# Weight blocks of a two-layer fp32 trunk: six of them split into a rounded part and its remainder by transfers instead of a subtraction on VectorE

## The chip, the cores and the metric

The kernel runs on one core of one Trainium2 chip. The metric is the device time of one execution in microseconds, as a median of several runs: 1206.23 us for the kernel before (three runs, 1202.98 to 1206.3 us). A profile is one further execution, recorded by the hardware profiler; every duration below is from that execution.

## The reference

A trunk of two layers works on x (512 positions by 1024 channels) and on a memory of 256 positions. Each layer has a mixer, an attention over the memory and a squared-ReLU MLP, each behind an RMS norm and added to x:

```python
mem_n = rms_norm(mem, mem_norm_g)
for l in range(2):
    h = rms_norm(x, mix_norm_g[l])
    x = x + (mixer_attn_rglru(h, ...) if l % 2 == 0 else pool_mixer(h, pool_w, scale))
    x = x + memory_xattn(rms_norm(x, xattn_norm_g[l]), mem_n, w_q, w_kv, q_g, k_g, w_o)
    x = x + jnp.square(jax.nn.relu(rms_norm(x, mlp_norm_g[l]) @ w1)) @ w2
```

The part of interest is layer 1. Its pooling mixer forms, in four groups of 256 channels, the mean over the last 2, 4, 8 or 16 positions minus the value itself, after which each group goes through a 256x256 matrix:

```python
window_sum = cs[:, 1:, sl] - cs[:, lo, sl]
diffs.append(window_sum / count - hf[..., sl])
out = jnp.einsum('bsgc,gcd->bsgd', d, pool_w)
```

The memory attention of the same layer needs k and v of the memory, `mem_n @ w_kv` with a weight of 1024 x 2048. This product doesn't depend on x, so it can be computed beside the mixer. All arithmetic is fp32.

## The kernel before

**Three products for one.** TensorE multiplies in a rounded fp32 type (fp32r). To keep fp32 accuracy, each operand is split into a high part (the value rounded to fp32r) and a low part (the value minus its high part), and `mm3` (L361) adds three matmuls: high x high, high x low, low x high. A weight comes from memory in blocks of 128 x 1024 fp32 (512 KB). `conv` (L427) splits a block: `split` (L383) has ScalarE (ACT) write the high part `wh` from the raw block, and then has VectorE (DVE) write the low part `wl` = `raw` - `wh`. An activation or norm operand is split in the same way (`xh`, `xl` and others).

**Buffers.** Raw blocks lie in a ring of 8 buffers that SP's queue fills (L394), each load waiting for the subtraction that frees its buffer. `wh` and `wl` have 5 buffers each; `block()` (L450), which TensorE's code calls for the next block, starts the split of the block that lies four further on. In the MLPs some raw blocks are added to others in memory: a transfer issued by GpSimd (POOL) with `accum_op=add` (L415), 128 of them in the program.

**Order.** The order on every engine is made when the program is built, and it is fixed: each engine takes its instructions one after the other, and each waits for the semaphores of what it reads or overwrites. The order comes from a small planner. Every operation asks for its engine (`yield ("dve", ...)`), and of those whose inputs are due soon, `tick` (L206) takes the one with the earliest due block; the table `DUE` (L20) holds how many blocks ahead of its use each kind of work is due.

**Layer 1 around the change.** `run` (L1490) sets the order of TensorE's blocks. Block numbers count weight blocks in the order in which TensorE takes them, from 0:

- blocks 173 to 176: the first quarter of `w_kv` (k of heads 0 and 1)
- blocks 177 and 178: the pooling matrices (`pool_mix`, L1436), 24 matmuls of 512 columns each
- blocks 179 to 190: the other three quarters of `w_kv` (`kv_group`, L1093), 12 matmuls of 512 columns each
- blocks 191 and on: the query projection, 24 matmuls each, which reads x after the mixer

While TensorE works through blocks 179 to 190, VectorE does what follows the pooling matrices for the eight tiles m = 0 to 7 of x: it scales the product (`z`), forms the window sums (`zs`, for m of 4 and more from a running sum `zc`), the difference `df`, adds it to `x`, and then splits the new x for the query projection: ScalarE writes `xh`, VectorE `xl` (L570). ScalarE and VectorE also square and add x for the next norm (`sq`), and finish k (`ksq`, `xss`, `xvv` and, over GpSimd's power `xrk`, `xkn`, which TensorE transposes into `kTh`, `kTl`) and v (`xvh`, `xvl`).

Of the kernel before, what the change touches and what calls it, by code (L numbers as in the profile page):

```python
# [6 lines left out]
F32 = mybir.dt.float32  # L7
F32R = mybir.dt.float32r
AF = mybir.ActivationFunctionType
ALU = mybir.AluOpType  # L10
# [6 lines left out]
WARM = 12  # L17
MM = 0.2162 / 512

DUE = {'xv': 0.3, 'xg': 2.6, 'xw': 4.9, 'evac_s': 0.6, 'form': 1.6, 'late': 2.5, 'stats_d': 2.31, 'exact': 0.32, 'q2': 8.88, 'conv': 1.47, 'evac': 1.41, 'norm': -1.9, 'sq': 3.08, 'stats': 0.76, 'xc0': 9.87, 'xc1': 1.14, 'gate0': 17.89, 'gate1': 1.73, 'kt': 15.09, 'qt': 13.77, 'dil0': 15.42, 'dil1': 2.26, 'lru': 6.84, 'pool0': 131.7, 'pool1': 1.91, 'soft': 2.17, 'kvt': -0.68, 'mem': 32.21, 'o': 2.22, 'conv_d': 0.31, 'mem_d': 56.21, 'lam_d': 2.23}  # L20
LOOK = 0.33
BACK = 0.46
TABLE = 1.28
# [22 lines left out]
def weight_blocks():  # L46

    out = []

    def cols(name, l, c0, k0=0, nk=4):  # L50
        for j in range(nk):
            out.append((name, l, k0 + 256 * j, c0))

    cols("ev_w_in", 0, 1536)
    cols("ev_w_in", 0, 512)
    cols("ev_w_in", 0, 0)
    out.append(("gates", 0, 0, 0))
    cols("ev_w_in", 0, 1024)
    cols("ev_w_in", 0, 2048)

    def kv(l, g0, g1):
        for g in range(g0, g1):
            cols("xa_w_kv", l, 512 * g)

    def two(name, l):
        cols(name, l, 0)
        cols(name, l, 512)

    def mlp(l):
        for c in range(4):  # L70
            for g in range(2):
                for i, j in S_RAWS:
                    out.append(("s:mlp_w1", l, 512 * j, 1024 * c + 512 * g + 256 * i))
            for g in range(2):
                for i, j in S_RAWS:
                    out.append(("t:mlp_w2", l, 1024 * c + 256 * j, 512 * g + 256 * i))

    kv(0, 0, 4)
    two("ev_w_out", 0)
    two("xa_w_q", 0)  # L80
    two("xa_w_o", 0)
    mlp(0)
    kv(1, 0, 1)
    out.append(("pool", 0, 0, 0))
    out.append(("pool", 0, 1, 0))
    kv(1, 1, 4)
    two("xa_w_q", 1)
    two("xa_w_o", 1)
    mlp(1)
    return out  # L90
# [5 lines left out]
def weight_units():  # L96


    out = []
    b, at = 0, 0.0  # L100
    blocks = weight_blocks()
    while b < NBLK:
        if blocks[b][0][1] == ":":
            for f in FORMS:
                for g in range(2):
                    out.append((b + 4 * g, f, at, 4 / 7))
                    at += 4 / 7
            b += 8
        else:
            out.append((b, None, at, 1))  # L110
            at += 1
            b += 1
    return out


UNITS = weight_units()


def weight_loads():


    out = []
    for b, form, _, _ in UNITS:
        if form in (None, "11"):
            out.append((b, (b, form), None))
        elif form == "a":
            out.append((b + 1, (b, form), b + 2))
        elif form == "c":
            out.append((b + 1, (b, form), b))
        elif form in ("12", "22"):  # L130
            out.append((b + (3 if form == "12" else 2), (b, form), None))
    return out


LOADS = weight_loads()
ACCUM = 7.9


class Trunk:
# [96 lines left out]
    def due_at(self, block):  # L236
        self.cur[1] = block
# [161 lines left out]
    def dma_next(self):  # L399

        if self.n_dma < len(LOADS) and self.n_raw < RAW_BUFS - 1:
# [6 lines left out]
            if more is not None:  # L408
                u = self.unit_at[key]
                self.spawn(self.accum(raw, more, f"F{u}"), UNITS[u][2] - DUE["conv"])  # L410

# [11 lines left out]
    def raw_free(self):  # L423
        self.n_raw -= 1
        self.dma_next()

    def conv(self, u):  # L427

        b, form, _, _ = UNITS[u]
        if form in ("a", "b", "c", "d"):  # L430
            yield f"F{u}"
        src = self.raw[b, {"b": "a", "d": "a"}.get(form, form)]
        hi = self.p_w.tile([128, 1024], F32R, tag="wh", name="wh")
        lo = self.p_w.tile([128, 1024], F32R, tag="wl", name="wl")
        self.w[u] = (hi, lo)
        if isinstance(src, list):
            for k in range(2):
                c = slice(512 * k, 512 * k + 512)
                yield from self.split(hi[:, c], lo[:, c], src[k])
        else:  # L440
            yield from self.split(hi, lo, src)
        self.mark(f"w{u}")
        if form in ("a", "b"):

            self.spawn(self.accum(src, b + (0 if form == "a" else 3), f"F{u + 4}", hi, lo),
                       UNITS[u + 4][2] - DUE["conv"])
        elif not isinstance(src, list):
            self.raw_free()

    def block(self):  # L450

        u = self.unit
        self.unit += 1
        self.blk = UNITS[u][2] + UNITS[u][3]
        if self.n_conv < len(UNITS):
            n = self.n_conv
            self.spawn(self.conv(n), UNITS[n][2] - DUE["conv"], DUE["conv_d"])
            self.n_conv += 1
        self.need(f"w{u}")
        return self.w.pop(u)  # L460


    def gemm_t(self, xs, evac, between=None, groups=2, nkb=4, tail=None):


        for g in range(groups):
            ps = [None] * 4
            for j in range(nkb):
# [5 lines left out]
                for m, k in order[:6] if last else order:  # L474
# [11 lines left out]
                    if kk == 2 * nkb - 1:  # L486
                        self.spawn(evac(4 * g + m, ps[m]), self.blk - DUE["evac"])
                    self.tick()
# [17 lines left out]
    def gemm_s(self, ops, evac, tail=None):  # L506
# [6 lines left out]
        for form in FORMS:  # L513
            for g in range(2):
# [22 lines left out]
                if not last:  # L537
                    self.spawn(evac(g, form, ps, gid), self.blk - DUE["evac_s"])

# [5 lines left out]
    def gemm_n(self, xs, nt, evac, nkb=4):  # L545

        ps = [None] * nt
        for j in range(nkb):
            wh, wl = self.block()
            for t in range(nt):  # L550
                if j == 0:
                    ps[t] = self.acc()
                for k in range(2):
# [6 lines left out]
                    if kk == 2 * nkb - 1:  # L560
                        self.spawn(evac(t, ps[t]), self.blk - DUE["evac"])
                    self.tick()
# [1025 lines left out]
```

## Time and profile before

| what | us |
|---|---|
| median of the runs | 1206.23 |
| the profiled execution, its own time | 1208.11 |
| its span, first to last instruction | 1206.3 |
| TensorE (PE) busy | 1186.3 |
| weight loads into TensorE (PEld) busy | 1093.1 |
| VectorE (DVE) busy | 931.9 |
| ScalarE (ACT) busy | 666.8 |
| GpSimd (POOL) busy | 148.8 |

The profiled execution's own time is 1.8 us above its span. Busy shares are averages over stages; what a stage waits for is read from the rows of that stage. A busy time of TensorE counts matmuls that run at a lower granted clock as busy too.

### The profile page before, as it was taken

How to read it: one execution, taken by the hardware profiler on the slowest of the kernel's cores; microseconds unless marked ns; L12 is line 12 of the kernel's file. 1: busy time of each engine (PE TensorE's matmuls, PEld its weight loads, DVE VectorE, ACT ScalarE, POOL GpSimd, SP SyncE). 2: the span in 40 equal slices, each digit the busy share in tenths (PEclk: the TensorE clock that was granted, in tenths of full speed). 3: DMA queues.
4: the chain of work that ended last, by engine and by line, in shares of the span. 5: the costliest groups of instructions: out<-in, count | busy, mean ns of one | idle time of the engine just before them, and what ended most of it. 6: DMA issues, size and time to landing. Idle time of an engine off the chain costs nothing.

```text
span 1206.3 us, 19988 instructions
## 1 busy us (share of the span) xinstructions
PE 1186.3 (98%) x7984; PEld 1093.1 (91%) x7984; DVE 931.9 (77%) x1419; ACT 666.8 (55%) x965; POOL 148.8 (12%) x172
## 2 busy tenths in 40 slices
PE   9999999999999999999999999999999999999998
PEld 6887888888889999999999977788899999999998
DVE  7959885555569877858958999946599869699697
ACT  6487764444456746436536657444476456465462
POOL 0110010010101111121211010001011211212110
PEclk9999999999999999999999999999999999999999
DMA  9223253322438699799899644433477998998984
GB/s 365 80 93 110 87 179 106 105 87 70 101 92 206 158 265 237 172 259 242 192 249 234 181 156 142 140 88 70 105 172 196 231 239 219 257 242 208 247 210 105
DMA packets 58989, 208.03 MB, mean 172 GB/s; under 512 B 6672, under 2 KB 7184, under 8 KB 58896
## 3 DMA queue, kind: packets, MB, share of 16 engines
q1 hardware_dynamic: 40320, 139.59, 33.2%
q0 software_dynamic: 18432, 67.12, 30.9%
q8 instruction: 62, 1.02, 0.3%
q14 instruction: 31, 0.25, 0.1%
q10 hardware_dynamic: 144, 0.05, 0.0%
HBM read 204.63 MB, written 2.10 MB: 171 GB/s over the span
## 4 chain that ended last, share of the span: by engine, by line
PE 81%; DVE 9%; ACT 4%; DMA 3%; issue 2%; POOL 0%; SPq 0%; DVEq 0%; ACTq 0%; POOLq 0%
PE acc L366 50%; PE misc L366 28%; DMA raw<-wpack 3%; DVE wl L274 3%; PE misc L373 1%; DVE p L274 1%; PE misc L379 1%; ACT wh L264 1%; DVE x L274 1%; DVE fl L274 1%; ACT sq L264 1%; DVE sq L274 1%; ACT xh L264 0%; DVE hs L274 0%; ACT a L264 0%
## 5 line engine op out<-in xcount | busy, mean ns | idle before, releaser
L264 ACT ACTIVATE wh<-raw 128x1024 fp32r<-128x1024 f32 (+1 forms) x321 | 333.4, 1049 | 297.2 <-PE acc L366 120.3
L274 DVE TENSOR_TENSOR wl<-raw,wh 128x1024 fp32r<-128x1024 f32 (+1 forms) x321 | 387.2, 1212 | 140.5 <-ACT wh L264 140.1
L415 POOL DMA_DIRECT2D raw<-wpack x128 | 111.2, 871 | 639.4 <-DVE wl L274 375.0
L366 PE MATMUL acc<-fh,wl 128*128 128x256 f32 x448 | 127.8, 285 | 3.7 <-DVE wl L274 3.7
L366 PE MATMUL acc<-fl,wh 128*128 128x256 f32 x448 | 127.6, 285 | 0.5 <-DVE x L274 0.5
L366 PE MATMUL misc<-fl,wh 128*128 128x256 f32 x448 | 127.1, 284 | 1.0 <-DVE fl L274 1.0
L366 PE MATMUL misc<-fh,wl 128*128 128x256 f32 x448 | 126.9, 283 | 0.8 <-DVE wl L274 0.8
L366 PE MATMUL acc<-fh,wh 128*128 128x256 f32 x448 | 127.5, 285 | 0.0
L366 PE MATMUL misc<-fh,wh 128*128 128x256 f32 x448 | 126.8, 283 | 0.0
L366 PEld LDWEIGHTS acc<-fh,wl 128*128 128x128 f32 x448 | 86.7, 194 | 4.3 <-DVE wl L274 4.3
L366 PEld LDWEIGHTS misc<-fl,wh 128*128 128x128 f32 x448 | 86.0, 192 | 1.6 <-DVE fl L274 1.6
L366 PEld LDWEIGHTS acc<-fl,wh 128*128 128x128 f32 x448 | 86.7, 193 | 0.7 <-DVE x L274 0.7
L366 PEld LDWEIGHTS misc<-fh,wl 128*128 128x128 f32 x448 | 86.0, 192 | 1.0 <-DVE wl L274 1.0
L366 PEld LDWEIGHTS acc<-fh,wh 128*128 128x128 f32 x448 | 86.6, 193 | 0.0
L366 PE MATMUL acc<-xh,wh 128*128 128x512 f32 x208 | 82.8, 398 | 3.4 <-ACT xh L264 2.2
L366 PEld LDWEIGHTS misc<-fh,wh 128*128 128x128 f32 x448 | 86.0, 192 | 0.0
L366 PE MATMUL acc<-xh,wl 128*128 128x512 f32 x208 | 82.1, 395 | 1.4 <-DVE wl L274 1.4
L366 PE MATMUL acc<-xl,wh 128*128 128x512 f32 x208 | 82.5, 397 | 0.8 <-DVE xl L274 0.8
L366 PE MATMUL acc<-oh,wh 128*128 128x512 f32 x160 | 62.7, 392 | 0.7 <-ACT oh L264 0.7
L366 PE MATMUL acc<-oh,wl 128*128 128x512 f32 x160 | 62.8, 392 | 0.0
L366 PE MATMUL acc<-ol,wh 128*128 128x512 f32 x160 | 62.5, 391 | 0.2 <-DVE ol L274 0.2
L366 PE MATMUL acc<-wl,mh 128*128 128x512 f32 x128 | 50.8, 397 | 0.9 <-DVE wl L274 0.9
(288 smaller groups left out, 3212.2 us busy)
## 6 DMA issues: line engine op xcount, KB each, us to landing
raw<-wpack SPq DMA_DIRECT2D x253, 512.0 KB, 4.8
raw<-wpack POOLq DMA_DIRECT2D x128, 512.0 KB, 6.9
x<-xT SPq DMA_DIRECT2D x8, 256.0 KB, 5.6
outT<-x SPq DMA_DIRECT2D x6, 256.0 KB, 2.2
raw<-wpack SPq DMA_DIRECT2D x4, 256.0 KB, 4.9
memr<-memT SPq DMA_DIRECT2D x4, 256.0 KB, 3.8
cst<-cst SPq DMA_DIRECT2D x1, 617.0 KB, 6.8
outT<-x SPq DMA_DIRECT2D x4, 128.0 KB, 2.4
```

The source lines that it names most:

```text
L264: self.nc.scalar.activation(out, in_, func, **kw)
L274: getattr(self.nc.vector, fn)(out, *args, **kw)
L366: self.nc.tensor.matmul(out, a, b, start=start and i == 0, stop=stop and i == 2, skip_group_check=shared)
L373: self.nc.tensor.transpose(out, in_, self.ident)
L379: self.nc.tensor.matmul(ps[:, t:t + 1], sq[:, t * 128:t * 128 + 128], self.one, start=True, stop=True)
L415: self.nc.gpsimd.dma_start(out=raw, in_=self.ins["wpack"][b], accum_op=ALU.add)
```

## The change

Six of the twelve blocks 179 to 190 are split in another way. They are the blocks of `w_kv` in layer 1, from column 512 on, whose rows begin at 256 or 768: blocks 180, 182, 184, 186, 188 and 190, every other one.

For such a block, GpSimd's queue issues a transfer of the block from memory straight into `wh`, which rounds it to fp32r on the way. ScalarE then writes `wl` = -1 x `wh`, and a second transfer on GpSimd's queue adds the block from memory to `wl`, which leaves the block minus its high part. The raw ring, the load on SP's queue and VectorE's subtraction are not used for these blocks. The table DUE gets one more entry, `'direct': 3.0`, the lead in blocks with which the planner counts these splits as due (1.47 for the others).

```diff
+def direct(block):
+
+    name, l, r0, c0 = block
+    return name == "xa_w_kv" and l == 1 and c0 >= 512 and r0 % 512 == 256
+
+
 def weight_loads():
...
+    blocks = weight_blocks()
     for b, form, _, _ in UNITS:
         if form in (None, "11"):
-            out.append((b, (b, form), None))
+            if not direct(blocks[b]):
+                out.append((b, (b, form), None))
...
+    def put(self, out, b, ins, key=None, **kw):
+
+        yield ("pool", ins)
+        self.nc.gpsimd.dma_start(out=out, in_=self.ins["wpack"][b], **kw)
+        t = max([self.free["dma"], self.T] + [self.due[r.tensor.name][0] for r in ins])
+        self.free["dma"] = max(self.free["dma"], self.T) + 524288 / 360e3
+        self.free["pool"] = max(self.free["pool"], self.T) + 0.9
+        self.due[out.tensor.name] = (t + ACCUM, "dma")
+
+    def conv_direct(self, u, b):
+
+        hi = self.p_w.tile([128, 1024], F32R, tag="wh", name="wh")
+        lo = self.p_w.tile([128, 1024], F32R, tag="wl", name="wl")
+        self.w[u] = (hi, lo)
+        yield from self.put(hi, b, [])
+        yield from self.A(lo, hi.bitcast(F32), AF.Copy, scale=-1.0)
+        yield from self.put(lo, b, [lo], accum_op=ALU.add)
+        self.mark(f"w{u}")
+
     def conv(self, u):
 
         b, form, _, _ = UNITS[u]
+        if form is None and direct(weight_blocks()[b]):
+            yield from self.conv_direct(u, b)
+            return
...
-            self.spawn(self.conv(n), UNITS[n][2] - DUE["conv"], DUE["conv_d"])
+            b, form = UNITS[n][:2]
+            lead = DUE["direct"] if form is None and direct(weight_blocks()[b]) else DUE["conv"]
+            self.spawn(self.conv(n), UNITS[n][2] - lead, DUE["conv_d"])
```

The planner puts the instructions around these blocks in another order. On **VectorE**, the piece that ends with the first update of x tile m = 2 (`x1_86<-df_...`; `x0_85` before it is m = 0 and 1). Before, with the subtractions of blocks 185 and 186 (`wl_7504`, `wl_7531`) in it:

```order
L274 TENSOR_REDUCE xss_7543<-ksq_7546 128x2
L274 TENSOR_TENSOR zs_7515<-z_7388 128x511
L274 SCALAR_TENSOR_TENSOR xvv_7544<-xss_7543,m_e_1400 128x2
L274 TENSOR_REDUCE xss_7558<-ksq_7561 128x2
L274 SCALAR_TENSOR_TENSOR xvv_7559<-xss_7558,m_e_1400 128x2
L274 SCALAR_TENSOR_TENSOR xl_7542<-x0_85,vec_83,xh_7541 128x512
L274 TENSOR_TENSOR zs_7556<-zs_7515 128x510
L274 TENSOR_TENSOR zs_7556<-zs_7556,cst_84 128x4
L274 TENSOR_TENSOR wl_7504<-raw_7347,wh_7503 128x1024
L274 SCALAR_TENSOR_TENSOR df_7595<-zs_7556,z_7388 128x512
L274 TENSOR_TENSOR wl_7531<-raw_7403,wh_7530 128x1024
L274 SCALAR_TENSOR_TENSOR x1_86<-df_7595,vec_83,x1_86 128x512
```

Now the same piece, with the subtraction of block 185 (`wl_7520`) and the two reductions of k's squares (`xss`) behind the update:

```order
L282 TENSOR_TENSOR zs_7494<-z_7388 128x511
L282 SCALAR_TENSOR_TENSOR xl_7509<-x0_85,vec_83,xh_7508 128x512
L282 TENSOR_TENSOR zs_7515<-zs_7494 128x510
L282 TENSOR_TENSOR wl_7520<-raw_7261,wh_7519 128x1024
L282 TENSOR_TENSOR zs_7515<-zs_7515,cst_84 128x4
L282 SCALAR_TENSOR_TENSOR df_7545<-zs_7515,z_7388 128x512
L282 SCALAR_TENSOR_TENSOR x1_86<-df_7545,vec_83,x1_86 128x512
L282 TENSOR_TENSOR sq_7501<-sq_7501,sq_7524 128x512
L282 TENSOR_TENSOR zs_7547<-z_7407 128x511
L282 SCALAR_TENSOR_TENSOR xl_7552<-x1_86,vec_83,xh_7551 128x512
L282 TENSOR_REDUCE xss_7562<-ksq_7565 128x2
L282 TENSOR_REDUCE xss_7576<-ksq_7579 128x2
```

Between the subtraction of block 179 and this update of x, both included, VectorE's list had eight subtractions before (blocks 179 to 186) and has four now (179, 181, 183, 185).

On **ScalarE**, the split of block 184: before, its high part (`wh_7479`) came early, ahead of the first new `xh`.

```order
L264 ACTIVATE wh_7459<-raw_7277 128x1024
L264 ACTIVATE wh_7479<-raw_7309 128x1024
L264 ACTIVATE zs_7486<-z_7374 128x1
L264 ACTIVATE wh_7503<-raw_7347 128x1024
L264 ACTIVATE zs_7515<-z_7388 128x1
L264 ACTIVATE xh_7508<-x0_85,vec_83 128x512
```

Now ScalarE's part of block 184 is the negated copy `wl_7484`, and it stands behind the `xh` of x tile m = 2. (`wh_7459` is block 183 and `wl_7411` the copy of block 182.)

```order
L272 ACTIVATE wh_7459<-raw_7239 128x1024
L272 ACTIVATE zs_7469<-z_7374 128x1
L272 ACTIVATE wl_7411<-wh_7410 128x1024
L272 ACTIVATE xh_7487<-x0_85,vec_83 128x512
L272 ACTIVATE zs_7494<-z_7388 128x1
L272 ACTIVATE sq_7501<-x0_85 128x512
L272 ACTIVATE xh_7508<-x0_85,vec_83 128x512
L272 ACTIVATE zs_7515<-zs_7494 128x2
L272 ACTIVATE wh_7519<-raw_7261 128x1024
L272 ACTIVATE sq_7524<-x0_85 128x512
L272 ACTIVATE xh_7551<-x1_86,vec_83 128x512
L272 ACTIVATE wl_7484<-wh_7483 128x1024
```

The last of the six copies, `wl_7689` of block 190, stands in the same way behind the `xh` of tile m = 5 (the second `xh<-x2_87`), and also behind the high part of block 192 (`wh_7753`):

```order
L272 ACTIVATE wh_7727<-raw_7347 128x1024
L272 ACTIVATE xh_7731<-x2_87,vec_83 128x512
L272 ACTIVATE sq_7750<-x2_87 128x512
L272 ACTIVATE wh_7753<-raw_7403 128x1024
L272 ACTIVATE wl_7689<-wh_7688 128x1024
```

Each of these copies is followed by an adding transfer on GpSimd's queue, which TensorE's low matmuls of the block wait for. GpSimd's list had four `xrk` and nothing else in this stretch; now twelve transfers stand among them.

## Rows read from the trace of the kernel before

**Rows 1.** The page: span and busy times; us, share of the span, instructions.
```profile
span 1206.3 us, 19988 instructions
PE 1186.3 (98%) x7984; PEld 1093.1 (91%) x7984; DVE 931.9 (77%) x1419; ACT 666.8 (55%) x965; POOL 148.8 (12%) x172
```
**Rows 2.** Windows: stretch and length, busy us and count of PE, PEld, DVE, ACT, POOL.
```profile
720.00:740.00 20.00, 20.00 (x94) 16.57 (x93) 18.82 (x31) 15.59 (x27) 1.83 (x2) 1.00 0.50 158
740.00:760.00 20.00, 17.68 (x76) 13.62 (x75) 19.89 (x27) 10.86 (x16) 0.00 (x0) 1.00 0.41 132
```
**Rows 3.** Timeline of PE: start, duration, then [idle before it <- releaser].
```profile
742.89 0.39 PE L366 MATMUL acc<-wh,mh 128*128 128x512 f32 x1
743.72 0.50 PE L366 MATMUL acc<-wl,mh 128*128 128x512 f32 x1 [0.44 <-DVE wl L274]
...
747.24 0.50 PE L366 MATMUL acc<-wl,mh 128*128 128x512 f32 x1 [0.51 <-DVE wl L274]
...
754.62 0.50 PE L366 MATMUL acc<-xh,wl 128*128 128x512 f32 x1 [1.38 <-DVE wl L274]
...
773.11 0.50 PE L366 MATMUL acc<-xh,wh 128*128 128x512 f32 x1 [1.63 <-ACT xh L264]
774.16 0.50 PE L366 MATMUL acc<-xl,wh 128*128 128x512 f32 x1 [0.54 <-DVE xl L274]
```
**Rows 4.** Windows, PE alone: stretch, length, busy us (count), granted clock, DMA share, GB/s.
```profile
488.00:491.00 3.00, 1.00 (x9) 1.00 0.00 0
492.00:496.00 4.00, 4.00 (x23) 0.57 0.81 142
678.00:680.00 2.00, 0.33 (x4) 1.00 0.00 0
680.00:684.00 4.00, 4.00 (x34) 1.00 0.67 192
771.00:775.00 4.00, 1.83 (x8) 1.00 0.53 153
775.00:779.00 4.00, 4.00 (x12) 0.57 0.69 238
```
**Rows 5.** Timeline of PE: first matmuls of blocks 179 and 184.
```profile
717.47 0.39 PE L366 MATMUL acc<-wh,mh 128*128 128x512 f32 x1
...
731.07 0.39 PE L366 MATMUL acc<-wh,mh 128*128 128x512 f32 x1
```
**Rows 6.** Timeline of DVE, 715 to 756 us.
```profile
715.62 1.21 DVE L274 TENSOR_TENSOR wl<-raw,wh 128x1024 fp32r<-128x1024 f32 x1
716.75 0.68 DVE L274 TENSOR_TENSOR z<-acc,R 128x512 f32<-128x512 f32 x1
...
727.97 0.69 DVE L274 TENSOR_REDUCE xss<-ksq 128x2 f32<-128x512 f32 x1 [0.74 <-ACT ksq L264]
...
730.04 0.74 DVE L274 SCALAR_TENSOR_TENSOR xl<-x,vec,xh 128x512 fp32r<-128x512 f32 x1
...
734.47 0.74 DVE L274 SCALAR_TENSOR_TENSOR x<-df,vec,x 128x512 f32<-128x512 f32 x1
...
755.20 0.75 DVE L274 SCALAR_TENSOR_TENSOR x<-df,vec,x 128x512 f32<-128x512 f32 x1
```
**Rows 7.** Timeline of ACT.
```profile
717.49 1.06 ACT L264 ACTIVATE wh<-raw 128x1024 fp32r<-128x1024 f32 x1 [3.11 <-PE acc L366]
...
724.21 0.71 ACT L264 ACTIVATE xh<-x,vec 128x512 fp32r<-128x512 f32 x1
```
**Rows 8.** GpSimd's adding transfers, whole span: duration of the issue; time to landing.
```profile
L415 POOL DMA_DIRECT2D raw<-wpack x128: 862/862/1217, 285.6 to 1179.5; - x128
...
DMA to landing us min/median/max: 5.2/6.9/14.5
```
**Rows 9.** The same, the five that are issued from 640 to 700 us.
```profile
DMA to landing us min/median/max: 5.4/5.6/11.1
```
**Rows 10.** SP's raw loads, 680 to 800 us.
```profile
DMA to landing us min/median/max: 3.4/3.9/5.6
```

More of the change, by code (lines that the diff above doesn't have):

```diff
@@ L18 @@
 MM = 0.2162 / 512
-DUE = {'xv': 0.3, 'xg': 2.6, 'xw': 4.9, 'evac_s': 0.6, 'form': 1.6, 'late': 2.5, 'stats_d': 2.31, 'exact': 0.32, 'q2': 8.88, 'conv': 1.47, 'evac': 1.41, 'norm': -1.9, 'sq': 3.08, 'stats': 0.76, 'xc0': 9.87, 'xc1': 1.14, 'gate0': 17.89, 'gate1': 1.73, 'kt': 15.09, 'qt': 13.77, 'dil0': 15.42, 'dil1': 2.26, 'lru': 6.84, 'pool0': 131.7, 'pool1': 1.91, 'soft': 2.17, 'kvt': -0.68, 'mem': 32.21, 'o': 2.22, 'conv_d': 0.31, 'mem_d': 56.21, 'lam_d': 2.23}
+DUE = {'direct': 3.0, 'xv': 0.3, 'xg': 2.6, 'xw': 4.9, 'evac_s': 0.6, 'form': 1.6, 'late': 2.5, 'stats_d': 2.31, 'exact': 0.32, 'q2': 8.88, 'conv': 1.47, 'evac': 1.41, 'norm': -1.9, 'sq': 3.08, 'stats': 0.76, 'xc0': 9.87, 'xc1': 1.14, 'gate0': 17.89, 'gate1': 1.73, 'kt': 15.09, 'qt': 13.77, 'dil0': 15.42, 'dil1': 2.26, 'lru': 6.84, 'pool0': 131.7, 'pool1': 1.91, 'soft': 2.17, 'kvt': -0.68, 'mem': 32.21, 'o': 2.22, 'conv_d': 0.31, 'mem_d': 56.21, 'lam_d': 2.23}
 LOOK = 0.33
```

## The prediction, made before the changed kernel had run

> **What bounds the kernel now.** I read the page first: the span is 1206.3 us and VectorE is busy 77% of it [rows 1]. An average says little about twelve blocks, so next came the windows by stage. From 740 to 760 us VectorE is busy 19.89 of 20 us, while TensorE, which has work all the time, is busy only 17.68 [rows 2]. So in this stage, and in few others, VectorE sets the pace.
>
> The timeline of TensorE shows what that costs. Five matmuls come late: two low matmuls of blocks 188 and 189, one of block 191, and two that wait for the last split of x [rows 3]. Their idle times add to 0.44 + 0.51 + 1.38 + 1.63 + 0.54 = 4.5 us. Each costs a bit more than its idle: the first pair starts 0.83 us apart, where such matmuls stand 13.60 / 60 = 0.227 us apart (blocks 179 to 183, five blocks of 12, fill 717.47 to 731.07 [rows 5]); 0.83 - 0.227 - 0.44 = 0.16 us more. With that for all five the stage loses 5.3 us.
>
> There is a second loss behind it. After TensorE has idled most of 771 to 775 us, the mean granted clock of 775 to 779 is 0.57 of full speed [rows 4], so it ran most of that stretch at 1.2 GHz instead of 2.4: 4 x (1 - 0.57) = 1.7 us are lost. The same happens after an idle of 2.00 us within 488 to 491 us (0.57 in 492 to 496) and doesn't after 1.67 us within 678 to 680 (1.00 in 680 to 684) [rows 4]. I carry 1.7 us for a wait as long as the two that were followed by it. What the stage loses now: 5.3 + 1.7 = 7.0 us. That is all that a change in this stage can win, if nothing takes its place.
>
> **What the change removes.** Six subtractions of VectorE. One occupies it for 716.75 - 715.62 = 1.13 us (its row shows 1.21, so 0.08 overlap the next; a row of 512 elements, 0.68, occupies it for 0.6) [rows 6]. Together 6.8 us, more than the 5.3 us by which it is late. VectorE's lateness at blocks 188, 189 and 191 and at the last x should therefore go: the whole 7.0 us. Six raw loads leave SP's queue, so its ring reaches further ahead; I found no row of ScalarE in this stage that a load releases, and count nothing.
>
> **What it adds without cost.** Six negated copies replace six high parts on ScalarE, both 128 x 1024 (1.06 us [rows 7]): no difference in busy time. Twelve issues of 0.86 us [rows 8] are 10.3 us for GpSimd, which does 1.83 us of work in 720 to 740 [rows 2]; the `xrk` pair that stands behind block 184's adding transfer has inputs that are themselves later now, so it hides. GpSimd's next powers come after the last of the twelve.
>
> **What it adds on the path: the way to `wl`.** Before, a low part needed ScalarE, then VectorE, some 2.3 us after the raw block was there. Now it needs a rounding transfer, the copy, and an adding transfer, one after the other, and all three stand in queues that take their work in order. The price of an adding transfer, from issue to landing: the fastest of 128 took 5.2 us, their median is 6.9 [rows 8], and the five issued last before this stage have 5.6 [rows 9]. I take 5.8, a little over the nearest row, since twelve more transfers join here. No row shows a rounding transfer: a plain load from SP needs 3.4 us at best [rows 10], an adding one 6.9. Both ends give the same, as the copy behind it waits longer for something else, as follows.
>
> *Block 182* tells how near this runs. Its copy stands behind the high part of block 183, which waits for TensorE to finish block 178, at 717.49 [rows 7]. Copy done 717.49 + 1.06 + 1.06 = 719.6; add landed at 725.4. TensorE wants it one matmul into block 182, at 717.47 + 3 x 2.72 + 0.23 = 725.9. It holds, by 0.5 us.
>
> *Block 184* doesn't. Its copy stands on ScalarE behind `xh` of x tile 2, which waits for VectorE to update that tile. This update started at 734.47 [rows 6]. Four of the subtractions ahead of it go (4 x 1.13 = 4.5 us), and the two `xss` with their wait move behind it: from about 727.2 (727.97 less its wait of 0.74) to 730.04, less one `zs` of 0.6 that stays, 2.2 us [rows 6]. So it starts at 734.47 - 6.7 = 727.8 and ends at 728.5. Then `xh` (0.71) and the copy (1.06 [rows 7]): issue at 730.3. The rounding transfer for this block can be issued right after block 182's add at 719.6 and has landed by 727.4 even at 6.9 us, so it is not what ends last. The add lands at 730.3 + 5.8 = 736.1. TensorE, which nothing else delays, wants it at 731.07 + 0.23 = 731.3 [rows 5]. **TensorE waits 4.8 us**, longer than any wait it has now, and by the rows on the clock pays **1.7 us** more.
>
> *Blocks 186 and 188.* After the wait, block 184 has 11 matmuls left (2.5 us), and the transposes of k (0.9: blocks 184 to 187 took 742.89 - 731.07 = 11.8 us [rows 3, 5], of which four times 2.72 are matmuls). So 185 starts at 739.5 and 190 at 739.5 + 5 x 2.72 = 753.1. The copies for 186 and 188 come to ScalarE at about 735 and 741, so their adds land at about 742 and 748, within 0.7 us of TensorE's need on either side; the 1.7 us of slow clock cover that.
>
> *Block 190* is late again. Its copy stands behind `xh` of tile 5, whose x update was at 755.20, 20.7 us after that of tile 2 [rows 6]. Between the two, three subtractions go (-3.4); the `xss` pair and its small followers come in (+1.3) with one `sq` more (+0.6), one `xvl` moves out (-0.7); and VectorE idles some 1.0 us at k's `kTl`: its transposes stand on TensorE behind the wait at block 184, so with a copy by ScalarE its input is there at 738, and VectorE by the same count at 737. So 727.8 + 18.5 + 1.0 = 747.3, ended 748.0; then `xh`, `sq`, block 192's high part and the copy, by [rows 7] 0.71, 0.6, 1.06 and 1.06 less the overlaps, some 3.2: issue at 751.2, landed 757.0. TensorE wants it at 753.1 + 0.23 + 1.7 = 755.0. **Wait 2.0 us**, and just long enough for **1.7 us** of clock again.
>
> **Sum.** Lost now in this stage 4.8 + 1.7 + 2.0 + 1.7 = 10.2 us, before 7.0: 3.2 us slower. Behind it VectorE has slack (its last x is some 6 us earlier while TensorE is later), and TensorE is the bound, so the 3.2 us go through to the end: 1208.1 + 3.2 = 1211.3 on the profiled execution's scale. The median of the runs lies 1.9 us lower, so 1209.4.
>
> A page speaks against the price that I took. The Trainium skill ("DMA: Bandwidth & Descriptors", Anatomy of one DMA — SWDGE (gpsimd) path) gives a transfer issued by GpSimd as about 2.0 us plus its bytes over 436 GB/s, by estimate 3.2 us for 512 KB. No adding transfer of this trace comes near that: the fastest of 128 needed 5.2. By the page block 184 would wait 2.2 us instead of 4.8; the nearest row that would give such a time is the plain load, which is the second rival.
>
> **Rivals.**
> - *The transfers are slower than the nearest row.* Over the whole span the median add takes 6.9 us, and single ones up to 14.5 [rows 8]. From about 6.3 us block 182 begins to wait, and each microsecond more is paid at block 184 and again at 190, as its copy is late by the idle at `kTl` too. At 6.9: 1.1 x 2 = 2.2 us more plus 0.6 at block 182, so 6.0 us slower, 1212.2; at 8 us 4.4 + 1.7 more, 9.3 us slower, 1215.5. For it: six adds also convert to fp32r, which no row shows, and raw loads share the queues. Against: this stage has the lightest transfer load (share 0.41 to 0.50 [rows 2]).
> - *A GpSimd transfer lands like a plain load*, 3.4 us. Then block 184 waits 730.3 + 3.4 - 731.3 = 2.4 us, clock 1.7; block 190 starts 2.4 us sooner (752.6 with the clock), VectorE has no idle at `kTl`, the add lands at 750.2 + 3.4 = 753.6: wait 1.0. Together 5.1 against 7.0: 1204.3. Against it stand 128 adds of 5.2 us or more.
> - *The relief carries (faster).* If VectorE reaches tile 2's update 3 to 5 us before my sum, block 184's copy is bound by its rounding transfer alone: landed about 725.5, copy, add, 732.4: wait 1.1, no drop, and nothing at block 190. That is 6 us faster, 1200.3. For it: VectorE is the named releaser of most waits. Against: the order fixes what stands ahead of the update.
> - *That the change doesn't do what it says*: the built order has the six subtractions gone and the twelve transfers in, so this is left only as a case with no difference.
>
> **How the numbers follow.** The forecast (adds landing in 5.4 to 6.3 us, 1.5 to 5 us slower; 1207.7 to 1211.2) gets 0.55. A change of less than 0.3%, 3.6 us, can't be told from none here; the bound to slower is 1209.85, so the forecast sits just within, and I give 0.33 of it to no difference and 0.22 to slower. Slow transfers 0.20 (slower). Landing like a plain load 0.12 (0.08 same, 0.04 faster, by the spread of the runs, 3.3 us). The relief 0.09 (faster). No effect 0.04 (same). Faster 0.13, same 0.45, slower 0.42. The range leaves out the relief below and the worst of slow transfers above: 1203.2 to 1215.5.
>
> **What would show it.** Right: a PE row `acc<-wl,mh` that idles 4 to 5.5 us before block 184's second matmul, near 736 us, released by a DMA into `wl`; a shorter one near 757; the clock near half for some microseconds after the first; the five waits of [rows 3] gone; adding transfers at 5.4 to 6.3 us. Wrong: a wait below 3 us at block 184, waits still named after VectorE, or PE busy throughout.

## The result, and the profile after

| | before | after |
|---|---|---|
| median of the runs, us | 1206.26 (1202.98 to 1206.73, six) | 1214.49 (1211.49 to 1215.73, six) |
| ratio to before | 1 | 1.007 (95% interval 1.0055 to 1.0086) |
| the profiled execution, us | 1208.11 | 1214.86 |

The change made the kernel slower by 8.2 us, 0.7%. The forecast was 1209.4, 3.2 slower; the time is inside the range, but it belongs to the first rival, which had a chance of 0.20 ("the transfers are slower than the nearest row": 1212.2 at a landing of 6.9 us, 1215.5 at 8).

The page of after, answering to [rows 1]:

```profile
span 1213.1 us, 19992 instructions
PE 1187.8 (98%) x7984; PEld 1093.8 (90%) x7984; DVE 926.5 (76%) x1413; ACT 666.2 (55%) x965; POOL 157.9 (13%) x184
```

VectorE lost its six subtractions (1419 to 1413 instructions, 5.4 us less busy), and the span grew by 6.8. The execution of before came 2.2 us later to the stage in question, so I measure the stage by itself, between two TensorE rows that every version has: the matmuls of `r`, just ahead of the pooling matrices, and the first scores of the attention behind the query projection (columns as in [rows 3]). Before:

```profile
702.41 1.16 PE L677 MATMUL misc<-cst,r 128*128 128x128 f32 x8 [0.66 <-POOL r L296]
794.12 0.28 PE L366 MATMUL misc<-kTh,qh 128*128 128x256 f32 x1
```

After:

```profile
700.19 1.16 PE L709 MATMUL misc<-cst,r 128*128 128x128 f32 x8 [0.66 <-POOL r L304]
800.99 0.28 PE L374 MATMUL misc<-kTh,qh 128*128 128x256 f32 x1
```

The stage took 91.71 us and now takes 100.80: **9.1 us more: the stage holds the whole loss** (from the scores to the end of the span both executions take 412.1 to 412.2 us). The late matmuls of TensorE from block 179 on, which answer to [rows 3], are the second matmuls of blocks 180, 182, 184, 186 and 190:

```profile
718.62 0.50 PE L374 MATMUL acc<-wl,mh 128*128 128x512 f32 x1 [0.22 <-DMA wl<-wpack]
726.53 0.50 PE L374 MATMUL acc<-wl,mh 128*128 128x512 f32 x1 [2.13 <-DMA wl<-wpack]
734.46 0.50 PE L374 MATMUL acc<-wl,mh 128*128 128x512 f32 x1 [0.57 <-DMA wl<-wpack]
744.27 0.52 PE L374 MATMUL acc<-wl,mh 128*128 128x512 f32 x1 [3.17 <-DMA wl<-wpack]
761.26 0.50 PE L374 MATMUL acc<-wl,mh 128*128 128x512 f32 x1 [4.21 <-DMA wl<-wpack]
```

Not one is released by VectorE or ScalarE any more; all five wait for an adding transfer. The granted clock fell behind three of them (windows of TensorE, columns as in [rows 4]):

```profile
727.00:731.00 4.00, 4.00 (x13) 0.57 0.59 190
744.00:748.00 4.00, 3.73 (x9) 0.58 1.03 235
761.00:765.00 4.00, 3.74 (x10) 0.59 0.69 251
```

That gives the sum again: waits of 10.3 us, some 0.8 around them (0.16 each, as in the prediction), and 4 x (0.43 + 0.42 + 0.41) = 5.0 us of clock are 16.1, against 7.0 before: 9.1.

GpSimd's timeline shows the issues (start, duration), of which six rows:

```profile
717.72 0.87 POOL L438 DMA_DIRECT2D wl<-wpack  x1 [5.88 <-DVE wl L282]
718.48 0.67 POOL L438 DMA_DIRECT2D wh<-wpack  x1
...
729.02 0.88 POOL L438 DMA_DIRECT2D wl<-wpack  x1 [3.99 <-ACT wl L272]
732.26 2.66 POOL L304 TENSOR_TENSOR xrk<-xvv,cst 128x2 f32<-128x2 f32 x2 [2.36 <-DVE xvv L282]
...
737.05 0.89 POOL L438 DMA_DIRECT2D wl<-wpack  x1 [1.58 <-ACT wl L272]
...
753.73 0.87 POOL L438 DMA_DIRECT2D wl<-wpack  x1 [11.00 <-ACT wl L272]
```

and the issues of the stage by tile, adding transfers and then rounding ones, the time to landing:

```profile
L438 POOL DMA_DIRECT2D wl<-wpack x6: 867/878/892, 710.9 to 753.7; - x6
DMA to landing us min/median/max: 5.4/7.5/8.8
```
```profile
L438 POOL DMA_DIRECT2D wh<-wpack x6: 548/600/889, 700.1 to 741.8; - x6
DMA to landing us min/median/max: 3.9/5.0/9.1
```

One by one the adds took 7.6, 8.8, 5.4, 7.2, 7.5 and 7.5 us, each issued 0.3 us behind the end of its copy (block 182's too, where the profile names a subtraction of VectorE that ended 0.2 us later than the copy). The longest is block 182's: a rounding transfer was issued right behind it at 718.48, and took 9.1.

### The profile page after: what moved, and what is told of

It reads as the page before. It is cut to its first block, busy times and chain, and to the rows that moved or that the text cites. A ratio compares the mean times of both kernels' runs of the same rounds, so it can differ in the third digit from the quotient of the medians.

```text
span 1213.1 us, 19992 instructions
## 1 busy us (share of the span) xinstructions
PE 1187.8 (98%) x7984; PEld 1093.8 (90%) x7984; DVE 926.5 (76%) x1413; ACT 666.2 (55%) x965; POOL 157.9 (13%) x184
## 4 chain that ended last, share of the span: by engine, by line
PE 82%; DVE 6%; DMA 5%; ACT 4%; issue 2%; POOL 0%; SPq 0%; DVEq 0%; ACTq 0%; POOLq 0%
PE acc L374 52%; PE misc L374 28%; DMA raw<-wpack 3%; DMA wl<-wpack 2%; DVE wl L282 2%; PE misc L381 1%; DVE p L282 1%; PE misc L387 1%; ACT wh L272 1%; DVE fl L282 1%; DVE x L282 1%; DVE hs L282 0%; ACT a L272 0%; PE misc L709 0%; ACT sq L272 0%
## 5 line engine op out<-in xcount | busy, mean ns | idle before, releaser
L282 DVE TENSOR_TENSOR wl<-raw,wh 128x1024 fp32r<-128x1024 f32 (+1 forms) x315 | 380.3, 1213 | 149.5 <-ACT wh L272 149.1
L272 ACT ACTIVATE wh<-raw 128x1024 fp32r<-128x1024 f32 (+1 forms) x315 | 327.2, 1049 | 303.5 <-PE acc L374 126.5
L374 PE MATMUL acc<-wl,mh 128*128 128x512 f32 x128 | 52.7, 412 | 10.3 <-DMA wl<-wpack 10.3
```

The source lines that it names most:

```text
L272: self.nc.scalar.activation(out, in_, func, **kw)
L282: getattr(self.nc.vector, fn)(out, *args, **kw)
L374: self.nc.tensor.matmul(out, a, b, start=start and i == 0, stop=stop and i == 2, skip_group_check=shared)
```

## The experiments

Theories, by the letters that the expectations use. **A**: the way to the low part (rounding, copy, add) is too long, and the adds land last. **B**: the new order of VectorE's and ScalarE's work is what makes TensorE late, whatever the transfers do. **C**: the twelve transfers and the raw loads slow each other. After four runs, A was split: **D**, the place of the copies in ScalarE's list alone; **E**, length and place together. "Stage" is always the stretch measured above. Idle time and stage are those of one profiled execution of each kernel, whose own time lay within 3 us of the median.

| kernel | blocks split by transfers | idle on adds, us | stage, us | ratio to before (95% interval) |
|---|---|---|---|---|
| before | none | 0 | 91.71 | 1 |
| after | six | 10.3 | 100.80 | 1.007 (1.0055 to 1.0086) |
| no adds | six | 0 | 92.72 | 1.0013 (1.0002 to 1.0025) |
| no rounding | six | 11.6 | 102.19 | 1.0076 (1.0058 to 1.0093) |
| block 188 | one | 5.4 | 91.27 | 1.0013 (1.0 to 1.0025) |
| block 188, early copy | one | 2.3 | 86.84 | 0.9973 (0.996 to 0.9986) |
| blocks 180 and 194 | two | 0 | 86.33 | 0.9948 (0.9934 to 0.9962) |
| early copies | six | 9.8 | 100.53 | 1.0074 (1.005 to 1.0098) |
| lead five, control | none | 0 | 93.24 | 1.0231 (1.0216 to 1.0246) |
| lead five | six | 5.3 | 90.38 | 1.0218 (1.0198 to 1.0238) |
| lead five, early copies | six | 0.9 | 90.13 | 1.0213 (1.0198 to 1.0228) |

### Without the adding transfers

```diff
-        self.nc.gpsimd.dma_start(out=out, in_=self.ins["wpack"][b], **kw)
+        if not kw:
+            self.nc.gpsimd.dma_start(out=out, in_=self.ins["wpack"][b], **kw)
```

> This kernel leaves out the six adding transfers, so the low parts of the six blocks are the negated copies alone; the order of everything else is that of the changed kernel. Theory A (the way to the low part is too long: rounding transfer, copy, adding transfer, one after the other, and the adds land last): the three TensorE waits released by a DMA into wl (2.1, 3.2 and 4.2 us idle) and the clock drops behind them are gone, and with them most of the 11 us of waits and 4.9 us of clock; what stays is one or two waits that the new order makes by itself (estimate 2 to 6 us). Time 1198 to 1204 us, 10 to 16 us below the changed kernel. Theory B (the new order of VectorE's and ScalarE's work makes TensorE late, whatever the transfers do): waits now named after ACT or DVE take the place of those named after a DMA, TensorE loses 9 us or more in 715 to 800 us, and the time stays at 1208 us or above. Theory C (twelve transfers and the raw loads slow each other): without the adds the rounding transfers land in 3.9 to 5.1 us, none at 8 to 9, and the raw loads fall back to 3.4 to 5.6 us.

Measured: 1207.6 us. TensorE's waits from 690 to 800 us (total, times, longest):

```profile
PE misc L381 <- ACT xkn L272: 3.2, 2, 2.1
PE acc L374 <- DVE xvl L282: 1.8, 1, 1.8
```

The clock was 0.59 in 732 to 736, where TensorE was busy for 2.44 us, and 0.56 in 736 to 740, so it cost 2.44 x 0.41 + 4 x 0.44 = 2.8 us more. A was right that the waits on the DMA go, and wrong on the time (1198 to 1204); B was wrong as the explanation of the whole, but not of a part. The stage splits in two: the adds are worth 100.80 - 92.72 = 8.1 us, and the order that goes with them loses, even with no add to wait for, all that six subtractions less should have won (92.72 against 91.71). C was right on landings: rounding transfers without adds beside them took 3.9 to 4.8 us, and the ones of 8 and 9 are gone; the slowest raw load of the stage took 4.6 us, against 8.6 in after.

### Without the rounding transfers

```diff
-        self.nc.gpsimd.dma_start(out=out, in_=self.ins["wpack"][b], **kw)
+        if kw.pop("memset", False):
+            self.nc.gpsimd.memset(out.bitcast(F32), 0.0)
+        else:
+            self.nc.gpsimd.dma_start(out=out, in_=self.ins["wpack"][b], **kw)
...
-        yield from self.put(hi, b, [])
+        yield from self.put(hi, b, [], memset=True)
```

> This kernel leaves out the six rounding transfers: GpSimd writes zeros into wh in their place, so the high parts of the six blocks are zero. The adding transfers stay. Theory C (the two kinds of transfers slow each other on GpSimd's queue): alone, the adds land in 5.2 to 6 us instead of a median of 7.5, the waits at blocks 186 and 190 fall by 1.5 to 2 us each, and the time falls by 4 us or more, to 1210 or below. Theory A: an add by itself takes 7 us or so beside raw loads; the waits at blocks 184 to 190 stay within 1 us of those of the changed kernel, the one at block 182 (whose add was issued directly behind a rounding transfer, 8.8 us) shrinks at most, and the time is within 3 us of 1214.5. Theory B: no difference, 1214.5, but with waits named after ACT.

Measured: 1214.64 us, the time of after (the profiled execution took 1217.6). The late matmuls, now of blocks 182, 184, 188 and 190, and the adds' landing:

```profile
726.63 0.50 PE L374 MATMUL acc<-wl,mh 128*128 128x512 f32 x1 [1.49 <-DMA wl<-wpack]
735.57 0.80 PE L374 MATMUL acc<-wl,mh 128*128 128x512 f32 x1 [3.19 <-DMA wl<-wpack]
...
751.35 0.50 PE L374 MATMUL acc<-wl,mh 128*128 128x512 f32 x1 [1.02 <-DMA wl<-wpack]
762.95 0.80 PE L374 MATMUL acc<-wl,mh 128*128 128x512 f32 x1 [5.86 <-DMA wl<-wpack]
```
```profile
DMA to landing us min/median/max: 5.4/6.7/9.1
```

With half of the new transfers gone the adds are hardly faster, and the one of 9.1 us (block 190's, issued at 753.83) had no other transfer of GpSimd near it, only raw loads. So it isn't the rounding transfers that make the adds late, and C falls as the cause of after's time as far as the twelve go; that the raw loads do it was not tested. The other way round C holds: beside adds a rounding transfer took up to 9.1 us in after, without them at most 4.8. A's time was right; that each wait would stay within 1 us was not (0.57 became 3.19 at block 184, 3.17 went at 186). The copy of block 190 ran at 752.48 here, 6.3 us after its input, the zeros, was written: its place in ScalarE's list holds it.

### Block 188 alone

```diff
-    return name == "xa_w_kv" and l == 1 and c0 >= 512 and r0 % 512 == 256
+    return name == "xa_w_kv" and l == 1 and c0 == 1536 and r0 == 256
```

> Only block 188 is split by the two transfers; the other eleven go by the subtraction as before. With one of each kind, nothing else stands on GpSimd's queue beside them. Theory A: the chain of rounding, copy and add is too long for four blocks of 2.72 us even when it runs alone; TensorE waits 4 to 7 us at block 188, released by a DMA into wl, and the clock drops once (1.7 us); the other waits of the kernel before are mostly gone or pushed behind this one, and the time is 1204 to 1209 us. Theory C: a lone add lands in 5.2 to 5.8 us and a lone rounding transfer in 4, there is no wait above 2 us, and the time is 1199 to 1203. Theory B: within 2 us of the kernel before.

Measured: 1207.36 us, and A's wait. The time by itself would fit B too (1.25 us above the kernel before); the wait tells them apart. The two issues on GpSimd, the copy on ScalarE, and the matmul that waits:

```profile
729.66 0.62 POOL L438 DMA_DIRECT2D wh<-wpack  x1 [0.45 <-issue]
741.13 0.88 POOL L438 DMA_DIRECT2D wl<-wpack  x1 [10.86 <-ACT wl L272]
...
739.78 1.05 ACT L272 ACTIVATE wl<-wh 128x1024 fp32r<-128x1024 f32 x1
...
746.52 0.79 PE L374 MATMUL acc<-wl,mh 128*128 128x512 f32 x1 [5.37 <-DMA wl<-wpack]
```

The landings were 4.0 and 5.3 us, as C said for lone transfers; with the copy 4.0 + 1.05 + 5.3 = 10.4 us, a little less than four blocks of 2.72. The wait is there because the rounding had landed at 733.7 and the copy came at 739.8, 6.1 us later. That is where A had to be split into D and E.

### Blocks 180 and 194

```diff
+DIRECT = {weight_blocks()[u[0]]: True for i, u in enumerate(UNITS) if i in (180, 194)}
...
-    return name == "xa_w_kv" and l == 1 and c0 >= 512 and r0 % 512 == 256
+    return DIRECT.get(block, False)
```

> Only blocks 180 and 194 are split by the two transfers. Their four blocks of lead include blocks of 24 matmuls (177 and 178 ahead of 180; 191 and on ahead of 194), so that the chain has 16 to 20 us in place of 10.9. Theory A: the adds land in time, no TensorE wait is released by a DMA into wl, VectorE is still relieved of subtractions at its worst point, and the waits that the kernel before has there (5.3 us and 1.7 of clock) fall to about 1 us: 1199 to 1202 us, that is 0.995 to 0.997 of the kernel before. Theory B: waits named after ACT or DVE stay, and the time is 1205 or above. Theory C: with two adds 25 us or more apart and rounding transfers apart from them, adds land in 5.2 to 6 us.

Measured: 1199.74 us, ratio 0.9948, faster than both kernels. TensorE from 740 to 780 us (columns as in [rows 2]), and its clock in 776 to 780 (as in [rows 4]):

```profile
740.00:760.00 20.00, 20.00 (x89) 16.22 (x88) 20.00 (x30) 10.83 (x17) 1.46 (x2) 1.00 0.51 149
760.00:780.00 20.00, 20.00 (x95) 16.82 (x94) 15.26 (x25) 9.98 (x16) 3.00 (x3) 0.91 0.51 167
```
```profile
776.00:780.00 4.00, 4.00 (x13) 0.57 0.31 114
```

No wait on an add and none of the five of [rows 3]: two subtractions less, in the order that the planner makes with them, were enough, and no more is to be had here than the 1.7 us of clock. The adds took 7.3 and 6.0 us (C said 5.2 to 6), and the longer chain bears that, at block 180 only just: its copy ran at 708.40, 5 us after the rounding transfer had landed, the add landed at 717.0, and the load of its weights into TensorE waited 0.35 us, though no matmul counts as late.

### Early copies, lead of four

```diff
-        self.due[out.tensor.name] = (t + ACCUM, "dma")
+        self.due[out.tensor.name] = (t + (ACCUM if kw else 4.0), "dma")
```

> The changed kernel with one number of its planner changed: it books the landing of a rounding transfer at 4.0 us (measured with block 188 alone) in place of 7.9, so that it puts the negated copies earlier into ScalarE's list. The lead stays at four blocks. Theory D (the place of the copies alone: in the kernel with block 188 alone the rounding transfer had landed at 733.7 and the copy ran at 739.8, behind ten other instructions): the waits released by a DMA into wl fall from 10.3 to 3 us or less and the time to 1201 to 1205 us. Theory E (length and place together: four blocks, 10.9 us, are used up by rounding 4 to 5, copy 1 and add 5.5 to 7.5 as soon as anything stands between): one wait less, but waits of 2 and 4 us at blocks 188 and 190 stay with two clock drops, and the time is 1208 to 1212 us.

Measured: 1211.7 to 1215.1 us in three executions; a fourth, the profiled one, took 4576 us (its matmuls of 256 columns took 0.69 us on average in place of 0.28) and is left out. The same kernel ran again for its waits:

> The kernel with six blocks, a lead of four and early copies once more, for its waits: its time was that of the changed kernel, and its profiled execution couldn't be read. Theory E, now with adds at 7 us and more under the traffic of six blocks: waits released by a DMA into wl of 8 to 11 us in total, at blocks 184, 188 and 190, with two or three clock drops, 1211 to 1216 us. If instead the waits on the DMA are below 5 us and waits named after ACT or DVE make up the rest, it is the order of the other work that the early copies push back.

Measured: 1214.02 us, with blocks 182, 184, 188 and 190 late:

```profile
725.74 0.50 PE L374 MATMUL acc<-wl,mh 128*128 128x512 f32 x1 [0.48 <-DMA wl<-wpack]
735.09 0.50 PE L374 MATMUL acc<-wl,mh 128*128 128x512 f32 x1 [3.58 <-DMA wl<-wpack]
...
754.37 0.50 PE L374 MATMUL acc<-wl,mh 128*128 128x512 f32 x1 [3.37 <-DMA wl<-wpack]
762.43 0.50 PE L374 MATMUL acc<-wl,mh 128*128 128x512 f32 x1 [2.32 <-DMA wl<-wpack]
```

The waits on adds come to 9.8 us, and only 0.65 is named after ScalarE (`xkn`). D falls for six blocks. E's first range of time was 2 to 3 us too low, and its second was right for a reason that was not: the adds didn't land at 7 us and more, but the rounding transfers did. Adds, then rounding transfers:

```profile
DMA to landing us min/median/max: 5.3/5.9/7.2
```
```profile
DMA to landing us min/median/max: 4.7/7.4/7.9
```

From block 182 on every copy now starts when its rounding transfer has landed, so its place costs nothing any more. But four of these transfers stand directly behind the add of an earlier block in GpSimd's list: they are issued only when that block's copy is done, and they took 6.2 to 7.9 us beside its add, not the 4.0 that was booked. Here the two kinds do slow each other, and C has a part in E's length.

### Block 188 alone, early copy

The two edits above together.

> Only block 188 by transfers, as before, and the landing of its rounding transfer booked at 4.0 us in place of 7.9, so that its copy stands earlier in ScalarE's list. If the copy's place made block 188 late (the rounding had landed at 733.7, the copy ran at 739.8, and TensorE waited 5.4 us), then the wait released by a DMA into wl falls to 0 to 2 us, no clock drop follows, some 1 to 2 us of waits on VectorE come back at blocks 189 and 191, and the time is 1202 to 1205 us, 2 to 5 below the kernel with block 188 alone. If the length of the chain made it late by itself, the wait stays at 4 us or more and the time within 1.5 us of that kernel.

Measured: 1202.3 us. The copy and the matmul:

```profile
737.19 1.05 ACT L272 ACTIVATE wl<-wh 128x1024 fp32r<-128x1024 f32 x1
...
745.37 0.50 PE L374 MATMUL acc<-wl,mh 128*128 128x512 f32 x1 [2.26 <-DMA wl<-wpack]
```

Counted from the start of the stage, 2.0 us later here, the copy runs 4.6 us earlier than in the kernel with the late copy; the add took 6.8 us instead of 5.3, and the wait fell by 3.1. No clock drop followed (1.00 in 745 to 749), and the stage is 4.4 us shorter. The wait is a little above the 2 us that the expectation allowed, and no wait on VectorE came back at blocks 189 and 191. For one block, the copy's place decides.

### Lead of five, with and without early copies, and the control

```diff
-SLOTS, RAW_BUFS, W_BUFS = 55, 8, 5
+SLOTS, RAW_BUFS, W_BUFS = 53, 7, 6
```

> The changed kernel with six buffers each for wh and wl in place of five (and seven raw ones, 53 slots of work space, to make room), so that the split of a block starts five blocks ahead of its use, not four: 13.6 us in place of 10.9. The booking stays at 7.9. Theory D: the copies stay behind the same work, and the time falls by no more than 3 us, to 1211 or above. Theory E: each wait released by a DMA into wl is up to 2.7 us shorter; 5 to 7 us of waits are left, at blocks 184 and 190, with one or two clock drops: 1204 to 1210 us.

> Both together: six buffers each for wh and wl, and the landing of a rounding transfer booked at 4.0 us. All six blocks by transfers, all twelve transfers in the same stretch. Theory E: no wait above 1 us is released by a DMA into wl, VectorE's relief shows, and the time is 1199 to 1203 us, faster than the kernel before. Theory D: as the kernel with early copies alone, within 2 us. Theory C (contention of twelve transfers and the raw loads sets the time): adds still land at 7 us and more, waits on them of 5 us in total or more stay, and the time is 1207 or above.

> The control: the kernel before, no block split by transfers, with the same six buffers each for wh and wl, seven raw buffers and 53 slots. If the buffers by themselves change nothing, as TensorE waits for VectorE there and not for the lead, the time is within 2.5 us of the kernel before, 1204 to 1208.7, and the five waits on VectorE and ScalarE of [rows 3] stay. If a longer lead is worth something by itself, the time is below 1203 and the gain of the kernel with both must be counted from here.

The times (1229.6, 1230.4 and 1232.0 us for the control) say nothing on the theories by themselves: the other buffer sizes cost all three 21 to 25 us ahead of this stage (it begins at 723 to 727 us in place of 702), a wait of 12.2 us for `vl` near 121 us among them. My expectation that buffers alone change nothing was wrong. The stage itself can be compared, with the control's 93.24. TensorE's waits in it with a lead of five:

```profile
PE acc L374 <- DMA wl<-wpack: 5.3, 3, 2.2
```

and with early copies as well:

```profile
PE misc L381 <- ACT xkn L272: 2.7, 2, 1.5
PE acc L374 <- DMA wl<-wpack: 0.9, 1, 0.9
```

Lead alone halves the waits on adds (10.3 to 5.3 us) and no clock drop follows them; lead and place together take nearly all. In the last, all twelve transfers still run in the stage, with adds of 5.4 to 7.3 us. So E stands for the waits: neither lead nor place is enough by itself to remove them for six blocks. For the time it doesn't: the lead alone gives 90.38 us, and early copies on top of it 90.13, because now k's `xkn` on ScalarE is late and the clock falls behind it (0.63 in 762 to 766). Against the control's 93.24 the six blocks win 2.9 and 3.1 us of the stage, and 2.3 and 1.6 of the median. Two blocks, 5.4 us below the kernel before, win more than six.

## Why the prediction was off

The direction, the kind of wait (TensorE's low matmuls, released by an adding transfer) and the range were right. The path was not: by the sign that the prediction itself named, "a wait below 3 us at block 184", it was wrong. The loss begins ahead of that block, at 182.

- **What bounds the stage before, 7.0 us, and that the change takes these five waits away:** right. None of them is left in after. VectorE's relief was right too: its update of tile 2 was forecast at 727.8, which is 725.6 on after's scale, and came at 726.08.
- **Block 182, "it holds, by 0.5 us":** wrong, by the landing. The copy was forecast to be done at 719.6, which is 717.4 on after's scale (2.2 us earlier); it was done at 716.37 + 1.05 = 717.4. The add was issued 0.3 us behind it and landed 8.8 us after that, not 5.8; TensorE waited 2.13, and its clock fell.
- **Block 184, a wait of 4.8 us:** the issue was forecast at 728.1 on that scale and came at 729.02; the add took 5.4. TensorE had already lost time at block 182 and in the slow clock behind it, so 0.57 was left. The wait was moved, not avoided.
- **The price of a rounding transfer, "both ends give the same":** only just, and from outside both ends. Block 184's took 9.1 us and landed at 727.6, as the `xh` ahead of the copy ended.
- **Block 186, within 0.7 us:** wrong; the wait was 3.17. I had counted that the `xrk` pair hides on GpSimd. But ScalarE's `xkn` waits for it, and the copy stands behind `xkn`. The pair is late because block 182 was: k's squares `ksq` wait on ScalarE until TensorE ends that block, some 4 us later than it would have without its wait and slow clock (2.13 + 0.16 + 1.7), and `xss`, `xvv`, `xrk` and `xkn` follow one another from there (timeline of ScalarE in after):

```profile
730.79 0.60 ACT L272 ACTIVATE ksq<-acc 128x512 f32<-128x512 f32 x1 [1.58 <-PE acc L374]
...
733.51 0.84 ACT L272 ACTIVATE xkn<-acc,xrk 128x256 f32<-128x256 f32 x2 [0.57 <-POOL xrk L304]
734.95 0.84 ACT L272 ACTIVATE xkn<-acc,xrk 128x256 f32<-128x256 f32 x2 [0.60 <-POOL xrk L304]
735.68 1.06 ACT L272 ACTIVATE wl<-wh 128x1024 fp32r<-128x1024 f32 x1
```

  The copy came 2.9 us later than my 735 (732.8 on after's scale), and the add took 7.2.
- **Block 190, a wait of 2.0:** right in place and cause, 4.21 in size; 1.7 of the difference is the landing, 7.5 instead of 5.8. The rest nearly cancels: the issue came 4.7 us later than forecast, and TensorE 4.3 us later.
- **Clock, 1.7 us for each long wait:** right in price (1.6 to 1.7), and three times instead of two.

The term that was mis-sized is the landing of an adding transfer: 5.8 us in the sum, 5.4 to 8.8 with a median of 7.5 in after. The 5.8 came from the median of five [rows 9], among which one took 11.1. The reason given for a quick landing, a light transfer load, was read from before: the DMA share there was 0.40, 0.50 and 0.41 in the three windows of 20 us from 700, and the change raised it to 0.69, 0.81 and 0.76. That this traffic is what made the adds late is not shown: with the same twelve transfers in another order (early copies) their median was 5.9, and without the rounding ones 6.7.

The first rival's own sum, 2 us for each microsecond of landing and block 182 from 6.3 on, gives 1.7 x 2 + 1.2 = 4.6 us more at 7.5, which is 7.8 slower; measured 8.2. That it comes so near is in good part luck. It has TensorE wait 6.5 us at block 184, where 0.57 were measured, nothing at block 186, where it was 3.17, and two stretches of slow clock where there were three.

## What to carry to other kernels

A chain of two transfers with a copy between them is to be costed against the lead of its buffers, with landings as far apart as they are measured (5.3 to 9.1 us here) and not at the median of a few, and with the place of the copy and of both transfers in their engines' lists; a unit that is relieved helps nothing while another wait ends last. In this kernel such a split paid for few blocks, where the lead holds long work: two blocks won 0.5%, and six lost 0.7%.

## What the runs showed of the hardware

**Landing and traffic.** The profiles of these kernels hold 34 adding transfers of 512 KB into `wl` (the execution of 4576 us left out). Where the DMA engines were busy less than 80% between issue and landing (15 of them), the median was 5.5 us (5.3 to 7.6); above that (19), 7.3 (5.3 to 9.1). A slow transfer itself fills such a window, so the split shows that they go together, not how much the traffic causes. The Trainium skill ("DMA: Bandwidth & Descriptors", Queues, rings and completion order) has each DMA engine take turns between the queues that have work for it. The later landings beside raw loads would fit that, but no run here shows the turns. The estimate of 3.2 us by the Trainium skill ("DMA: Bandwidth & Descriptors", Anatomy of one DMA — SWDGE (gpsimd) path), named in the prediction, was met by none of the 34.

**A rounding transfer behind an add.** Eleven rounding transfers of the kernels with six blocks were issued on GpSimd less than 1 us behind an adding one; they took 5.9 to 9.1 us, with a median of 7.7. The ten of the kernels that had no add under way beside them (no adds, block 188 with late and early copy, blocks 180 and 194) took 3.9 to 4.9.

**The clock behind a wait.** How long TensorE waited does not by itself tell whether its clock falls. After 2.13 us (after, 726.5) it fell, after 2.26 (block 188, early copy) it didn't. In the kernel with six early copies it stayed at 1.00 behind a wait of 3.37 us and fell behind one of 2.32:

```profile
755.00:759.00 4.00, 4.00 (x19) 1.00 0.63 148
...
763.00:767.00 4.00, 4.00 (x12) 0.57 0.49 147
```

And in the kernel with blocks 180 and 194 it fell to 0.57 at 776 to 780 with no wait at all: what TensorE did before it, from 773 to 776, was 24 matmuls of one column each (`sq`, `qsq`) with two wide ones between them. What decides it stays open here.
